# Sums of activations for w_down's Strassen parts, made in gate and up and kept in DRAM

## The chip, the cores and the metric

The kernel runs on one core of one Trainium2 chip. The metric is device time in microseconds of that core, from start to end of one execution; several executions are timed and their median is given. The engines of the core run side by side, each with its own instruction stream: PE (TensorE, the matrix products), DVE (VectorE), ACT (ScalarE), POOL (GpSimd) and SP (SyncE, which here only issues transfers). ACT and POOL issue transfers as well.

## The reference

One decoder layer on 512 tokens of width 2048, in float32: a mixer (attention and gated DeltaNet, gated and merged), then the channel mixer, then a last norm. The change concerns the channel mixer:

```python
D_MODEL = 2048; SEQ = 512
D_FF = ((8 * D_MODEL // 3 + 255) // 256) * 256      # 5632
...
        h = _rmsnorm(x, norm_ffn[l]) * (1.0 + sc_f) + sh_f
        gate, up = jnp.split(h @ w_gate_up[l], 2, axis=-1)
        x = x + gt_f * ((jax.nn.silu(gate) * up) @ w_down[l])
    return _rmsnorm(x, final_norm)
```

## The kernel before

**Products.** Every float32 operand is split into a rounded high part and a remainder (`hilo` for activations, the loops over `his` and `los` for weights): ACT casts to the high part (L242, L1718), DVE subtracts it (L243, L1721), and a product takes three matmuls: high by high, high by low, low by high. In what follows "xh" and "xl" are the two parts of an activation operand, "hi" and "lo" those of a weight.

**Order of the work.** The program is a list of units. A unit has loads (`load`, on SP), a split (the casts and subtractions of its weights), matmuls, and small calls ahead and behind (`pre`, `post`). `Driver.run` takes them in turn. Beside them run chains: Python generators that are advanced one step per 12 matmuls (`GROUP = 12`, `Driver.pump`), or until a condition holds when a unit's `pre` needs their result (`ready`, `Driver.step`). PE, SP and POOL keep the order in which the program is written; ACT and DVE are put in order by the scheduler, other than those instructions that are wrapped in `behind`, which keep the written order. `load` issues on SP, `side` on POOL. All activation tiles of 128x512 come from one pool of 68 slots, "raws" (weights as loaded, and their sums) from a pool of 5, `his` and `los` from 4 each, PSUM has 8 banks.

**Gate and up.** Hidden columns come in sets. Sets 0 and 1 are plain (`gu0`, `gu_both`); sets 1 to 10 of `big` are Strassen products (`strassen`), 16 units each. In the first half (units 0 to 7) a unit has 24 matmuls, of the products m1, m6, m7 and m5; in the second half (units 8 to 15) 18, of m2, m4 and m3 (four of these units also have four transposes). A first-half unit loads three weight tiles, DVE makes three sums (`sums`, L1698), ACT casts and DVE subtracts; one of the loaded tiles is kept in `s_dram` for the second half by a transfer that ACT issues (L1720). The sums of the next unit are made in the same step and overwrite the tile that this transfer reads. The activation operands x5, x6, x7 and x3 of gate and up are sums that the chain `combine` makes during `gu_both`. The outcome, silu(gate)·up transposed, goes to `f_dram` (`turned_a`, by POOL) for 32 of the 44 blocks of 128 hidden columns, in tiles of 128x512 that hold two blocks of one half of the tokens; blocks 36 to 39 stay in slots and 32 to 35 and 40 to 43 go to `a_dram` in two parts. The chain `gated_weights` makes the gated weights of w_down for blocks 32 to 35 during the first sets: POOL loads a tile `wg`, DVE multiplies it with a row (L1897), it is split and stored in `l_dram`.

**Down.** Then w_down, in this order: `dn(36, n)` for n = 0 to 3 (plain, 192 matmuls in all), part 0 (`strassen_down(0, n)`, n = 0, 1, blocks 0 to 15), `dn(40, n)`, part 1 (`strassen_down(1, 0)` and `last_down`, which is `strassen_down(1, 1)` with 64 transposes of x2 in it), and last blocks 32 to 35 with the gated weights ("dnt": `last_set`, `token_unit`), the sum of squares and the norm. `dn_done` evicts the banks of a `dn` set with ACT ("y", L2066).

A part's seven activation operands per q (q = 0 to 3, two units of a half use one q) come from the chain `sums_down`: four tiles a11, a21, a22, a12 are loaded from `f_dram` on SP, four sums are made on DVE (L1983) and seven operands split. m1, m6, m7 and m5 are used in the first half, m2, m4 and m3 in the second. The chain is started at unit 10 of `big(10)` for part 0, and at unit 10 of `strassen_down(0, 1)` for part 1; `free(q)` lets it take the slots of q only when older operands are gone:

```python
        def free(q):
            return q < 4 and gone[ks] >= min(q + 2, 4) and (q < 3 or plain_sets[0] > 4 * ks + 3)
```

`reload_a(40..43)` brings blocks 40 to 43 back for `dn(40, n)`, eight POOL loads, at unit 10 of `strassen_down(0, 1)`. `last_weights(n)` loads eight "wl" tiles of the gated weights on SP; `last_rows` issues four POOL transfers that add z and four SP loads of the norm's rows.

Of the kernel before, what the change touches and what calls it, by code (L numbers as in the profile page):

```python
# [15 lines left out]
P = 128  # L16
# [155 lines left out]
def block_kernel(ctx: ExitStack, tc: tile.TileContext, a: dict, out):  # L172
# [65 lines left out]
    def hilo(src, name, scale=None):  # L238
        hi, lo = S(name + "h", F32R), S(name + "l", F32R)
        n = src.shape[1]  # L240
        if scale is None:
            nc.scalar.copy(hi[:, 0:n], src)  # L242
            nc.vector.tensor_tensor(lo[:, 0:n], src, hi[:, 0:n].bitcast(F32), ALU.subtract)  # L243
# [1043 lines left out]
    z_dram = dram.tile([NT, P, D], F32, name="z_dram")  # L1287
    l_dram = dram.tile([4, 4, 2, P, 512], F32, name="l_dram")
# [358 lines left out]
    def combine():  # L1647

        for q in range(4):
# [23 lines left out]
    def strassen(w, g, u, par, operand, ready, second_read, finish, freed, extra=None):  # L1673
# [53 lines left out]
        def pre(i):  # L1727
            ready(i % 8 // 2)
# [55 lines left out]
    def big(s):  # L1784
# [8 lines left out]
        def ready(q):  # L1793
# [37 lines left out]
    def strassen_down(ks, n, extra=None):  # L1831
# [3 lines left out]
        def ready(q):  # L1835
            while made[ks] <= q:
# [68 lines left out]
    turning = []  # L1905

    def turned_a(b):
# [3 lines left out]
        def one(n):  # L1911
# [11 lines left out]
            if n == 3:  # L1923
                if s < 8:
                    f_ = S("f")
                    nc.scalar.copy(f_[:], box["ps"][:])
                    side(f_dram[2 * s + b // 2, h], f_[:])
                else:
# [14 lines left out]
    down, made, maker = [[None] * 4, [None] * 4], [0, 0], [None, None]  # L1943
# [7 lines left out]

    def sums_down(ks):

        ahead = []

        def free(q):
            return q < 4 and gone[ks] >= min(q + 2, 4) and (q < 3 or plain_sets[0] > 4 * ks + 3)

        def fetch_a(q):
            v = {}  # L1960
            for name, i, h in (("a11", 8 * ks + q, 0), ("a21", 8 * ks + q, 1), ("a22", 8 * ks + 4 + q, 1), ("a12", 8 * ks + 4 + q, 0)):
                v[name] = S(name)
                load(v[name][:], f_dram[i, h])
                yield 2
            ahead.append(v)

        for q in range(4):
            if not ahead:
                yield from until(lambda: free(q))
                yield from fetch_a(q)  # L1970
                yield 5
            v = ahead.pop(0)
            more = free(q + 1)
            if more:
                fetching = fetch_a(q + 1)
            v["x7"] = S("x7")
            d = {}
            for c, dst, x, y, op in (("m7", "x7", "a11", "a21", ALU.subtract), ("m1", "a11", None, None, None),
                                     ("m5", "a21", "a22", "a21", ALU.subtract), ("m4", "a22", None, None, None),
                                     ("m6", "a11", "a11", "a21", ALU.add), ("m2", "a12", None, None, None),  # L1980
                                     ("m3", "a12", "a11", "a12", ALU.subtract)):
                if op is not None:
                    behind(nc.vector.tensor_tensor(v[dst][:], v[x][:], v[y][:], op))  # L1983
                d[c] = hilo(v[dst][:], "x")
                if op is None:
                    if more and next(fetching, None) is None:
                        more = False
                    yield
            v = None
            if more:  # L1990
                yield from fetching
            down[ks][q] = d
            made[ks] = q + 1
            yield
# [5 lines left out]
    def gu_done(s, ps):  # L2000
# [3 lines left out]
        def done(j, h):  # L2004
            if h == 0:
                return
            for h in range(2):
# [7 lines left out]
                if j == 3:  # L2015
                    side(f_dram[s, h], f[h][:])
        return done
# [59 lines left out]
    def ffn():  # L2077
# [77 lines left out]
        def last_down():  # L2155
            for i, u in enumerate(strassen_down(1, 1, turned_x2)):
# [173 lines left out]
```

## Time and profile before

| | us |
|---|---|
| median of 3 runs (2823.3 to 2823.59) | 2823.41 |
| the profiled execution | 2822.31 |
| its span, first to last instruction | 2820.5 |
| PE busy | 2737.4 (97%) |
| DVE busy | 2012.8 (71%) |
| ACT busy | 1136.7 (40%) |
| POOL busy | 245.8 (9%) |

The profiled execution has 1.8 us outside its span and lies 1.1 us under the median. PE's busy share is high throughout; the time between matmuls that waits for other engines is small beside it, and must be read stage by stage. The granted clock of PE is 1.00 in a full-speed stretch and 0.50 in a stretch at half speed.

### The profile page before, as it was taken

The numbers are of one execution on the slowest core, as the hardware profiler recorded it, in microseconds if no ns is written. First come the engines' busy times: TensorE is split into PE (matmuls) and PEld (weight loads), VectorE is DVE, ScalarE is ACT, GpSimd is POOL, SyncE is SP. The second block draws the span as 40 slices with busy tenths as digits, with TensorE's granted clock in tenths as the row PEclk, the third lists the DMA queues.
The fourth block names the chain that finished last, engine by engine and source line by source line (L and its number), as shares of the span: only waits on it lengthen the run. The fifth ranks groups of instructions, "written<-read, shape, count | busy, mean of one in ns | idle before, by whom it ended". The sixth has DMA issues, their size and how long they took to land. (4 is left out here: it accounts for less than half of the span.)

```text
span 2820.5 us, 37178 instructions
## 1 busy us (share of the span) xinstructions
PE 2737.4 (97%) x13478; PEld 2282.4 (81%) x13478; DVE 2012.8 (71%) x3114; ACT 1136.7 (40%) x1593; POOL 245.8 (9%) x324
## 2 busy tenths in 40 slices
PE   9999999999999999999999999999999997997987
PEld 7888788888888888888997888888888885785775
DVE  8784657676867456883678888777778858767754
ACT  3443333443344332232554444444444444344332
POOL 0000011002100000000001011000000020111033
PEclk9999999999999999999999999999999998998998
DMA  9896556546755468894656667656666686687697
GB/s 353 297 353 203 157 168 185 180 146 184 210 148 179 145 213 277 283 310 138 188 168 211 233 226 239 213 202 199 206 209 214 212 216 187 225 258 182 164 300 214
DMA packets 319969, 606.00 MB, mean 215 GB/s; under 512 B 42948, under 2 KB 79972, under 8 KB 319656
## 3 DMA queue, kind: packets, MB, share of 16 engines
q1 hardware_dynamic: 255544, 482.06, 52.9%
q0 software_dynamic: 27744, 63.23, 8.5%
q10 hardware_dynamic: 36496, 58.34, 5.7%
q8 instruction: 105, 1.72, 0.2%
q14 instruction: 80, 0.66, 0.1%
HBM read 505.97 MB, written 97.53 MB: 214 GB/s over the span
## 5 line engine op out<-in xcount | busy, mean ns | idle before, releaser
L267 DVE TENSOR_TENSOR lo<-raw,hi 128x1024 fp32r<-128x1024 f32 (+1 forms) x274 | 336.8, 1230 | 314.7 <-ACT hi L266 301.0
L266 ACT CAST hi<-raw 128x1024 fp32r<-128x1024 f32 (+1 forms) x274 | 285.1, 1042 | 676.4 <-DMA raw<-in_w_in_dram 133.8
L1718 ACT CAST hi<-raws 128x1024 fp32r<-128x1024 f32 (+1 forms) x336 | 302.1, 908 | 553.7 <-DVE raws L1698 268.0
L1721 DVE TENSOR_TENSOR lo<-raws,hi 128x1024 fp32r<-128x1024 f32 (+1 forms) x336 | 350.4, 1043 | 194.5 <-ACT hi L1718 192.9
L438 DVE CUSTOM_DVE_ANT_0 rawm<-rawm,cbc 128x1024 f32<-128x1024 f32 x192 | 233.8, 1236 | 10.8 <-DMA rawm<-in_w_mod_dram 10.6
L155 PE MATMUL m<-hi,xh 128*128 128x512 f32 x448 | 183.6, 410 | 29.6 <-ACT xh L242 26.8
L155 PE MATMUL m<-lo,xh 128*128 128x512 f32 x448 | 182.2, 407 | 10.1 <-DVE lo L1721 9.9
L155 PE MATMUL m<-hi,h2h 128*128 128x512 f32 x480 | 190.5, 397 | 0.0
L155 PE MATMUL m<-lo,h2h 128*128 128x512 f32 x480 | 187.4, 390 | 1.7 <-DVE lo L1721 1.6
L155 PE MATMUL m<-hi,xl 128*128 128x512 f32 x448 | 182.4, 407 | 5.4 <-DVE xl L243 5.3
L155 PE MATMUL m<-hi,h2l 128*128 128x512 f32 x480 | 187.2, 390 | 0.0
L1698 DVE TENSOR_TENSOR sums<-raws,raws 128x1024 f32<-128x1024 f32 x112 | 136.3, 1218 | 30.2 <-DMA raws<-in_w_down_dram 17.6
L1721 DVE TENSOR_TENSOR lo<-sums,hi 128x1024 fp32r<-128x1024 f32 x112 | 136.3, 1217 | 22.0 <-ACT hi L1718 21.9
L1718 ACT CAST hi<-sums 128x1024 fp32r<-128x1024 f32 x112 | 117.4, 1048 | 51.5 <-PE m L155 51.4
L155 PEld LDWEIGHTS m<-hi,xh 128*128 128x128 f32 x448 | 88.7, 198 | 51.4 <-ACT xh L242 30.2
L155 PEld LDWEIGHTS m<-lo,xh 128*128 128x128 f32 x448 | 88.9, 198 | 32.5 <-DVE lo L1721 13.9
L155 PE MATMUL wo<-mh,hi 128*128 128x512 f32 (+1 forms) x320 | 111.2, 347 | 0.0
L155 PE MATMUL wo<-mh,lo 128*128 128x512 f32 (+1 forms) x320 | 111.0, 347 | 0.0
L155 PE MATMUL wo<-ml,hi 128*128 128x512 f32 (+1 forms) x320 | 110.9, 347 | 0.0
L155 PEld LDWEIGHTS m<-hi,xl 128*128 128x128 f32 x448 | 88.0, 197 | 27.6 <-DVE xl L243 9.6
L155 PEld LDWEIGHTS m<-lo,h2h 128*128 128x128 f32 x480 | 90.3, 188 | 21.2 <-DVE lo L1721 3.6
L155 PEld LDWEIGHTS m<-hi,h2l 128*128 128x128 f32 x480 | 90.1, 188 | 19.2
(521 smaller groups left out, 6896.2 us busy)
## 6 DMA issues: line engine op xcount, KB each, us to landing
raws<-in_w_gate_up_dram SPq DMA_DIRECT2D x400, 256.0 KB, 3.6
rawm<-in_w_mod_dram SPq DMA_DIRECT2D x192, 512.0 KB, 5.5
raw<-in_w_in_dram SPq DMA_DIRECT2D x144, 512.0 KB, 4.6
raws<-in_w_down_dram SPq DMA_DIRECT2D x160, 256.0 KB, 5.1
s_dram<-raws ACTq DMA_DIRECT2D x112, 256.0 KB, 2.2
raws<-s_dram SPq DMA_DIRECT2D x112, 256.0 KB, 3.7
raw<-in_w_o_dram SPq DMA_DIRECT2D x40, 512.0 KB, 4.3
rawa<-in_w_in_dram SPq DMA_DIRECT2D x32, 512.0 KB, 4.1
```

The costliest lines, as they stand in the source:

```text
L155: return self.tc.keep_in_program_order(f(*args, **kwargs))
L266: nc.scalar.copy(hi[:], raw[:])
L267: (lo_eng or nc.vector).tensor_tensor(lo[:], raw[:], hi[:].bitcast(F32), ALU.subtract)
L438: r = nc.vector.tensor_tensor_reduce(raw, raw, c, 1.0, 0.0, ALU.mult, ALU.add, parts[:, k, half:half + 1])
L1698: add = lambda o, x, y: behind(nc.vector.tensor_tensor(o, x, y, ALU.add))
L1718: nc.scalar.copy(hi[:], src)
L1721: nc.vector.tensor_tensor(lo[:], src, hi[:].bitcast(F32), ALU.subtract)
```

## The change

The four sums of each q are made ahead, in a new chain `sums_ahead` that starts at unit 0 of `big(5)`: POOL loads a11, a21, a22, a12 from `f_dram` into slots as soon as they have been stored there, DVE makes the sum in the written order (`behind`), POOL stores it in a new DRAM tensor `c_sums`. Over both parts that is 32 POOL loads, 32 DVE sums and 32 POOL stores. The sums inside `sums_down` go; it now loads seven finished tiles per q on SP (56 loads instead of 32), splits them with the cast pinned to the written order (`late=True`), and does so in two groups: group 0 (m1, m6, m7, m5 of all q) and then group 1 (m2, m4, m3 of all q). A first-half unit waits for group 0 of its q, a second-half unit for group 1. The chain starts at unit 8 instead of 10, in both places.

Beside this, `reload_a(40..43)` moves from unit 10 of `strassen_down(0, 1)` to unit 13; `gated_weights` starts at unit 0 of `big(2)` instead of ahead of `big(1)`; `combine`'s casts are pinned and its step after each operand gives way once instead of twice; `last_weights(0..2)` come at units 10, 12, 14 instead of 11, 13, 15, and `last_weights(3)` is issued ahead of `last_rows` in the first "dnt" set instead of in the second. PE has 12576 rows in both kernels, ACT 1709, DVE 3004 and now 3005, SP 1360 and now 1384, POOL 307 and now 371.

```diff
-    def hilo(src, name, scale=None):
+    def hilo(src, name, scale=None, late=False):
...
-            nc.scalar.copy(hi[:, 0:n], src)
+            cast = nc.scalar.copy(hi[:, 0:n], src)
+            if late:
+                behind(cast)
...
             for name in ("x3", "x6", "x7", "x5"):
-                comb[q][name] = hilo(res.pop(name)[:], name)
-                yield 2
+                comb[q][name] = hilo(res.pop(name)[:], name, late=True)
+                yield
...
-        def ready(q):
-            while made[ks] <= q:
+        def ready(q, second):
+            while made[ks][second] <= q:
                 drv.step(maker[ks])
...
+    def sums_ahead():
+
+        for ks in range(2):
+            for q in range(4):
+                def get(i, h):
+                    assert (8 * ks + i, h) in stored
+                    v = S("a")
+                    side(v[:], f_dram[8 * ks + i, h])
+                    return v
+
+                def put(i, o, x, y, op):
+                    behind(nc.vector.tensor_tensor(o[:], x[:], y[:], op))
+                    side(c_sums[ks, q, i], o[:])
+
+                yield from until(lambda: all((8 * ks + i, h) in stored for i in (q, 4 + q) for h in range(2)))
+                a11, a21 = get(q, 0), get(q, 1)
+                yield 3
+                x7 = S("x7")
+                put(2, x7, a11, a21, ALU.subtract)
+                x7 = None
+                a22 = get(4 + q, 1)
+                yield 3
+                put(0, a21, a22, a21, ALU.subtract)
+                put(1, a11, a11, a21, ALU.add)
+                a22 = a21 = None
+                a12 = get(4 + q, 0)
+                yield 3
+                put(3, a12, a11, a12, ALU.subtract)
+                a11 = a12 = None
+                summed_ahead.add((ks, q))
+                yield 2
...
     def sums_down(ks):
...
+        def source(c, q):
+            if c in ("m1", "m2", "m4"):
+                return f_dram[8 * ks + (q if c == "m1" else 4 + q), int(c == "m4")]
+            return c_sums[ks, q, ("m5", "m6", "m7", "m3").index(c)]
+
+        queue = []
+
+        def make():
+            g, q, c, v = queue.pop(0)
+            down[ks][q][c] = hilo(v[:], "x", late=True)
+            if c in ("m5", "m3"):
+                made[ks][g] = q + 1
+
+        for g, cs in enumerate((("m1", "m6", "m7", "m5"), ("m2", "m4", "m3"))):
+            for q in range(4):
+                yield from until(lambda: gone[ks] >= (q if g == 0 else 4) and (g == 0 or q < 2 or plain_sets[0] > 4 * ks + 3))
+                for c in cs:
+                    assert (ks, q) in summed_ahead
+                    v = S("a")
+                    load(v[:], source(c, q))
+                    queue.append((g, q, c, v))
+                    v = None
                     yield
-            v = None
-            if more:
-                yield from fetching
-            down[ks][q] = d
-            made[ks] = q + 1
-            yield
+                    if len(queue) > 2:
+                        make()
+            while queue:
+                yield
+                make()
...
-                if i in (11, 13, 15):
-                    with_pre([u], lambda i=i: last_weights((i - 11) // 2))
+                if i in (10, 12, 14):
+                    with_pre([u], lambda i=i: last_weights((i - 10) // 2))
...
                 if n == 0:
-                    with_pre(us, last_rows)
-                else:
-                    with_pre(us, lambda: last_weights(3))
+                    with_pre(us, lambda: (last_weights(3), last_rows()))
...
-        drv.add(gated_weights())
         for s in range(1, 11):
             for i, u in enumerate(big(s)):
-                if (s, i) == (10, 10):
+                if s in (2, 5) and i == 0:
+                    with_pre([u], lambda s=s: drv.add(gated_weights() if s == 2 else sums_ahead()))
+                if (s, i) == (10, 8):
                     with_pre([u], lambda: maker.__setitem__(0, drv.add(sums_down(0))))
...
-                if (n, i) == (1, 10):
+                if (n, i) == (1, 13):
+                    with_pre([u], lambda: [reload_a(k) for k in range(40, 44)])
+                if (n, i) == (1, 8):
                     def start():
-                        for k in range(40, 44):
-                            reload_a(k)
                         maker[1] = drv.add(sums_down(1))
```

How the scheduler and the pools lay this out is seen in the instruction streams. In the rows a line number stands first, then the operation, the tile written, the tiles read and the size; "y" is the eviction of a `dn` set's bank, "xh" the high part of a part's operand, "hi" that of a weight.

ACT before, from the last work of `dn(36, 3)` into the first units of part 0:

```order
L242 CAST ah_20010<-aT_20005 128x512
L1718 CAST hi_20026<-raws_19865 128x1024
L1720 DMA s_dram<-raws_19865 128x512
L1718 CAST hi_20031<-sums_20020 128x1024
L242 CAST xh_20082<-x_3545_20080 128x512
L1718 CAST hi_20115<-raws_19917 128x1024
L242 CAST xh_20086<-a_3499_19892 128x512
L1720 DMA s_dram<-raws_19917 128x512
L2066 ACTIVATE y_20100<-dn_3_3533_20016,gt_ffn 128x512
L2066 ACTIVATE y_20103<-dn_3_3534_20017,gt_ffn 128x512
L2066 ACTIVATE y_20106<-dn_3_3535_20018,gt_ffn 128x512
L2066 ACTIVATE y_20109<-dn_3_3536_20019,gt_ffn 128x512
```

ACT now, the same place (the row "xh" is an operand of group 1; all sixteen casts of group 0 and three more of group 1 stand further ahead):

```order
L242 CAST ah_20218<-aT_20213 128x512
L1721 CAST hi_20234<-raws_20094 128x1024
L1723 DMA s_dram<-raws_20094 128x512
L1721 CAST hi_20239<-sums_20228 128x1024
L242 CAST xh_20264<-a_20129 128x512
L2093 ACTIVATE y_20300<-dn_3_3610_20224,gt_ffn 128x512
L2093 ACTIVATE y_20303<-dn_3_3611_20225,gt_ffn 128x512
L2093 ACTIVATE y_20306<-dn_3_3612_20226,gt_ffn 128x512
L2093 ACTIVATE y_20309<-dn_3_3613_20227,gt_ffn 128x512
L1721 CAST hi_20315<-raws_20131 128x1024
L1723 DMA s_dram<-raws_20131 128x512
L1721 CAST hi_20320<-sums_20231 128x1024
```

The four evictions of the last `dn` set stood behind two operand casts of part 0's second q; now no cast of a first-half operand stands near them.

ACT before, at the step from `gu_both` into `big(1)` ("sl" evicts the banks of `gu_both`, "wgh" is a split of `gated_weights`, x3h, x6h, x7h, x5h are `combine`'s last operands):

```order
L1720 DMA s_dram<-raws_12740 128x512
L242 CAST x3h_13009<-x_2163_13007 128x512
L1718 CAST hi_13119<-raws_12740 128x1024
L242 CAST x6h_13037<-x_2161_13003 128x512
L242 CAST wgh_13054<-wg_12987 128x512
L242 CAST x7h_13072<-x_2162_13005 128x512
L2012 ACTIVATE sl_13082<-gu_2082_12519 128x256
L2012 ACTIVATE sl_13084<-gu_2082_12519 128x256
L2012 ACTIVATE sl_13082<-gu_2083_12520 128x256
L2012 ACTIVATE sl_13084<-gu_2083_12520 128x256
L242 CAST x5h_13112<-x_2160_13001 128x512
```

ACT now, at the same place:

```order
L1723 DMA s_dram<-raws_12684 128x512
L1721 CAST hi_12971<-sums_12960 128x1024
L1723 DMA s_dram<-raws_12765 128x512
L1721 CAST hi_13091<-raws_12765 128x1024
L2038 ACTIVATE sl_13058<-gu_2082_12520 128x256
L2038 ACTIVATE sl_13060<-gu_2082_12520 128x256
L2038 ACTIVATE sl_13058<-gu_2083_12521 128x256
L2038 ACTIVATE sl_13060<-gu_2083_12521 128x256
L1721 CAST hi_13096<-sums_12963 128x1024
```

The evictions "sl" stood behind five casts, of three operands, a weight and a gated weight; now they stand behind one weight cast, and the operands' casts have moved ahead of it.

POOL before, between two stores of z, in the second half of `strassen_down(0, 1)`:

```order
L155 DMA z_dram<-y_20809 128x512
L155 DMA z_dram<-euvw 128x512 x4
L155 DMA ah_21249<-a_dram 128x512
L155 DMA al_21250<-a_dram 128x512
L155 DMA ah_21253<-a_dram 128x512
L155 DMA al_21254<-a_dram 128x512
L155 DMA ah_21257<-a_dram 128x512
L155 DMA al_21258<-a_dram 128x512
L155 DMA ah_21261<-a_dram 128x512
L155 DMA al_21262<-a_dram 128x512
L155 DMA row_21265<-g_dram 128x512
L155 DMA row_21267<-g_dram 128x512
```

POOL now:

```order
L155 DMA z_dram<-euvw 128x512 x4
L155 DMA row_21396<-g_dram 128x512
L155 DMA row_21398<-g_dram 128x512
L155 DMA ah_21523<-a_dram 128x512
L155 DMA al_21524<-a_dram 128x512
L155 DMA ah_21527<-a_dram 128x512
L155 DMA al_21528<-a_dram 128x512
L155 DMA ah_21531<-a_dram 128x512
L155 DMA al_21532<-a_dram 128x512
L155 DMA ah_21535<-a_dram 128x512
L155 DMA al_21536<-a_dram 128x512
L155 DMA z_dram<-y_21613 128x512
```

The eight reloads stood ahead of the two gate rows ("row", for `strassen_down`'s outcome) and now stand behind them; they were issued 126 matmuls and more ahead of `dn(40, 0)`, and now 39 to 14 matmuls ahead of it.

DVE before, in `big(5)` around the place where the first q is summed now:

```order
L1698 TENSOR_TENSOR sums_15978<-raws_15949,raws_15950 128x1024
L1721 TENSOR_TENSOR lo_15982<-raws_15904,hi_15981 128x1024
L1698 TENSOR_TENSOR raws_15949<-sums_15978,raws_15949 128x512
L1721 TENSOR_TENSOR lo_15987<-sums_15937,hi_15986 128x1024
L1721 TENSOR_TENSOR lo_16020<-raws_15949,hi_16019 128x1024
L1721 TENSOR_TENSOR lo_16025<-sums_15978,hi_16024 128x1024
L1698 TENSOR_TENSOR raws_15990<-raws_15990,raws_15991 128x512
```

DVE now, there:

```order
L1724 TENSOR_TENSOR lo_15918<-sums_15857,hi_15917 128x1024
L1970 TENSOR_TENSOR a_15791<-a_15851,a_15791 128x512
L1724 TENSOR_TENSOR lo_15960<-raws_15869,hi_15959 128x1024
L1970 TENSOR_TENSOR a_15789<-a_15789,a_15791 128x512
L1701 TENSOR_TENSOR sums_15956<-raws_15921,raws_15922 128x1024
L1724 TENSOR_TENSOR lo_15965<-sums_15909,hi_15964 128x1024
L1701 TENSOR_TENSOR raws_15921<-sums_15956,raws_15921 128x512
L1970 TENSOR_TENSOR a_15938<-a_15789,a_15938 128x512
L1724 TENSOR_TENSOR lo_16004<-raws_15921,hi_16003 128x1024
L1724 TENSOR_TENSOR lo_16009<-sums_15956,hi_16008 128x1024
```

Three operand sums (L1970) of the first q now stand between the weight sums and subtractions. The load that the third waits for, `a_15938`, is the POOL row after the second's store, 12 matmuls ahead of it in the program.

More of the change, by code (lines that the diff above doesn't have):

```diff
@@ L1287, in block_kernel @@
     z_dram = dram.tile([NT, P, D], F32, name="z_dram")
+    c_sums = dram.tile([2, 4, 4, P, 512], F32, name="c_sums")
     l_dram = dram.tile([4, 4, 2, P, 512], F32, name="l_dram")
@@ L1941, in kept_a @@
                 side(a_dram[k - 32, i], hl[i][:].bitcast(F32))
-    down, made, maker = [[None] * 4, [None] * 4], [0, 0], [None, None]
+    down, made, maker = [[{} for _ in range(4)] for _ in range(2)], [[0, 0], [0, 0]], [None, None]
     gone, plain_sets = [0, 0, 0], [0]
@@ L1950, in until @@
             yield
-    def sums_down(ks):
[L1954 to L1973, printed above, removed]
-            if more:
[L1975 to L1987, printed above, removed]
-                    yield
-            v = None
-            if more:
-                yield from fetching
-            down[ks][q] = d
-            made[ks] = q + 1
-            yield
```

9 lines of the change are left out of this document (6 added, 3 removed).

## The prediction

> **What bounds the kernel now.** I read the page first, then the waits of PE, then a table of stretches around each place that waits, and last the timeline there.
>
> ```profile
> PE 2737.4 (97%) x13478; PEld 2282.4 (81%) x13478; DVE 2012.8 (71%) x3114; ACT 1136.7 (40%) x1593; POOL 245.8 (9%) x324
> ...
> PE m L155 <- ACT xh L242: 26.8, 7, 6.6
> PE m L155 <- DVE lo L1721: 11.5, 10, 3.3
> PE dnt L155 <- DMA wl<-l_dram: 6.0, 5, 1.5
> PE m L155 <- DVE xl L243: 5.3, 6, 1.7
> PE m L155 <- ACT sl L2012: 5.2, 1, 5.2
> ...
> PE m L155 <- ACT y L2066: 2.7, 1, 2.7
> ```
>
> PE bounds the kernel; only stretches in which it waits can be won. The waits (total, times, longest) name two that the change touches at once: 26.8 + 5.3 us for operands of w_down's parts (xh, xl), and 5.2 us for the eviction "sl" at the entrance of the Strassen sets. What they cost with the clock that falls behind them is seen in the table of stretches: length, busy time of PE, PEld, DVE, ACT, POOL, granted clock, DMA share.
>
> ```profile
> 1889.03:1932.55 43.52, 43.52 (x194) 36.05 (x192) 37.36 (x43) 18.16 (x21) 0.00 (x0) 1.00 0.70 231
> 1490.11:1541.40 51.29, 46.00 (x194) 37.24 (x193) 40.75 (x50) 22.11 (x30) 5.57 (x11) 0.93 0.63 205
> 2324.87:2394.37 69.50, 53.25 (x194) 40.99 (x192) 55.30 (x69) 31.85 (x44) 6.08 (x6) 0.85 0.68 194
> 2427.01:2474.69 47.68, 44.70 (x194) 35.71 (x192) 36.81 (x42) 16.13 (x18) 9.10 (x17) 1.00 0.83 277
> 2550.85:2623.04 72.19, 53.46 (x194) 40.60 (x192) 52.23 (x66) 29.25 (x41) 5.16 (x6) 0.83 0.62 176
> 2655.68:2706.81 51.13, 46.09 (x193) 36.76 (x192) 37.86 (x43) 16.22 (x18) 9.34 (x13) 0.97 0.90 239
> 2754.60:2808.49 53.89, 47.85 (x195) 37.17 (x193) 24.89 (x61) 16.42 (x40) 22.28 (x22) 0.90 0.79 206
> ```
>
> All rows have 192 matmuls. The first, in set 6, has no wait and sets the measure: 43.52 us, or 0.2267 us a matmul. Against it the others have too much: the entrance of big(1) 7.8 us, the first half of part 0 26.0, of its second n 4.2, part 1 28.7 and 7.6, dnt 10.4. In the two long ones DVE works 55.30 and 52.23 us, more than 43.52: even with no wait for loads it could not keep up there, since twelve sums and twenty-one remainders are made inside.
>
> **Part 0 and part 1.** ACT at the head of part 0, then DVE and SP:
>
> ```profile
> 2327.55 0.62 ACT L242 CAST xh<-x 128x512 fp32r<-128x512 f32 x1 [5.72 <-DVE x L1983]
> ...
> 2329.75 1.83 ACT L2066 ACTIVATE y<-dn,gt_ffn 128x512 f32<-128x512 f32 x3
> ...
> 2340.19 0.62 ACT L242 CAST xh<-a 128x512 fp32r<-128x512 f32 x1 [4.05 <-DVE a L1983]
> ...
> 2339.47 0.68 DVE L1983 TENSOR_TENSOR a<-a,a 128x512 f32<-128x512 f32 x1
> 2340.07 0.69 DVE L1698 TENSOR_TENSOR raws<-sums,raws 128x512 f32<-128x512 f32 x1
> 2340.84 0.69 DVE L243 TENSOR_TENSOR xl<-a,xh 128x512 fp32r<-128x512 f32 x1
> ...
> 2334.51 2.21 SPq L155 DMA_DIRECT2D raws<-in_w_down_dram  x3
> 2336.81 2.54 SPq L155 DMA_DIRECT2D a<-f_dram  x3
> ```
>
> The eviction of the last dn set waits in ACT's order behind a cast that itself waited 5.72 us for a sum; PE stands 2.73 us. Later the sums wait for loads that SP issues only at 2336.81, behind three weight loads, and PE stands 6.10 us. Now the sums are gone, and all sixteen casts of group 0 stand ahead of the part. Their cover is the end of big(10) and dn(36, n):
>
> ```profile
> 2279.40:2324.90 45.50, 45.50 (x210) 37.64 (x209) 24.23 (x31) 20.86 (x31) 19.26 (x20) 1.00 0.95 229
> ```
>
> DVE works 24 of 45.50 us there, and sixteen remainders are 16 × 0.69 = 11 us, which fit. If that cover were gone, each operand would cost its wait again. Inside the first half DVE keeps 55.30 − 12 × 0.69 − 21 × 0.69 + 8 × 0.69 = 38 us (0.69 is the row of xl; twelve sums and 21 remainders go, eight remainders of group 1 come), under 43.52. SP issues 28 operand loads for a part instead of 16, but 16 of them ahead of it; twelve more at 0.85 us each (2.54 for three) are 10 us of SP's time, beside weight loads of 24 × 0.74 = 18 us (2.21 for three).
>
> What is late next are the weights: units overwrite the tile that the transfer into s_dram reads, and DVE waits for it.
>
> ```profile
> DVE sums L1698 <- DMA s_dram<-raws: 3.5, 3, 2.4
> ...
> L1698 DVE TENSOR_TENSOR sums<-raws,raws 128x1024 f32<-128x1024 f32 x112 | 136.3, 1218 | 30.2 <-DMA raws<-in_w_down_dram 17.6
> L1721 DVE TENSOR_TENSOR lo<-sums,hi 128x1024 fp32r<-128x1024 f32 x112 | 136.3, 1217 | 22.0 <-ACT hi L1718 21.9
> ```
>
> That wait stays. A unit has 24 matmuls, 5.44 us, and DVE needs 1.22 + 0.69 + 2 × 1.22 = 4.35 us for its weights, so a wait of 2.4 us leaves up to 1.3 us late, at two or three units: I leave 3 us of the 26.0 in part 0, and 3.7 of the 28.7 in part 1, which has the same form. Gains 23 and 25. Bounds: −26 and −28.7 if nothing is left; if only the DVE surplus goes (55.30 − 43.52 = 12, 52.23 − 43.52 = 9) and the rest stays, −12 and −9. I take values near the first end, since all 13 stands of xh and xl in PE's list lie in these two stretches, with y's as the one beside them.
>
> The second n of both parts, 4.2 and 7.6 us, waits for lo (11.5 us in the list) under busy DMA (0.83 and 0.90). Nothing there is taken away; the chain for part 1 begins two units earlier and casts earlier. 0, bounds −4 to +4.
>
> **Entrance of big(1).**
>
> ```profile
> 1497.52 1.20 ACT L2012 ACTIVATE sl<-gu 128x256 f32<-128x256 f32 x4
> 1468.64 0.69 DVE L1897 TENSOR_TENSOR wg<-wg,row 128x512 f32<-128x512 f32 x1 [10.05 <-DMA wg<-in_w_down_dram]
> 1460.99 0.55 POOL L155 DMA_DIRECT2D row<-g_dram  x1 [12.70 <-DMA g_dram<-gt_ffn]
> ```
>
> DVE stood 10.05 us for the first gated weight, whose row POOL could only fetch after a store; combine's sums came late behind it, its casts stood ahead of "sl", and PE waited 5.2 us and ran at half clock after it. With gated_weights in big(2) and the casts of x in front, sl stands behind one weight cast: −7.5 of 7.8, bounds 0 and −7.8. The 10.05 us hold does not return in big(2), where the store is long done.
>
> **Gate and up.** Added: 32 sums of 0.69 us on DVE, 64 transfers on POOL. Over four sets DVE has room, ACT and POOL more:
>
> ```profile
> 1889.03:2201.35 312.32, 312.32 (x1410) 258.57 (x1408) 245.16 (x285) 138.18 (x169) 10.81 (x20) 1.00 0.62 206
> ...
> f_dram<-f POOLq DMA_DIRECT2D x28, 256.0 KB, 2.6
> wg<-in_w_down_dram POOLq DMA_DIRECT2D x16, 256.0 KB, 4.5
> ah<-a_dram POOLq DMA_DIRECT2D x8, 256.0 KB, 8.8
> a<-f_dram SPq DMA_DIRECT2D x32, 256.0 KB, 5.1
> ```
>
> The sums are 22 us in some 470, DVE goes from 78% to 83% there. But a sum holds DVE in order until its load has landed. The shortest distance in the program is 12 matmuls, 2.7 us, against 4.5 us for a POOL load (wg) and 8.8 in a busier stretch (ah): a hold of 2 to 6 us at some six places (those with 12 to 22 matmuls between). A unit's weights are made two ahead, so about one unit, 5.4 us, is spare: +2, bounds 0 and +8. The two extra transfers of 256 KB per sum, 16.8 MB in all, are 36 GB/s beside 206.
>
> By the Trainium skill (DMA: Bandwidth & Descriptors, Anatomy of one DMA), a transfer issued by GpSimd takes about 2.0 us plus its bytes at 436 GB/s, an estimate of 2.6 us for 256 KB; by it this term would be 0 and the sum 2 us lower. The same page (Issuing engine by pattern) gives simple loads to Sync as the faster way, which speaks against this change; the rows above say 4.5 us by POOL and 5.1 by SP, so here neither is shown.
>
> **Reload.** Eight POOL issues of about 0.55 us, the last pair 14 to 18 matmuls ahead of dn(40, 0), whose first two blocks are needed at its start: 39 matmuls are 8.8 us, a landing 8.8 (ah above) after up to 2.2 us of issues. +1, bounds 0 (all lands) and +5 (the fourth load lands at 8.8 + 2.2 and loses clock). z's stores behind them are needed by nobody near.
>
> **dnt.** wl waits are 6.0 us, and 0.90 of clock costs the rest of 10.4. The first three sets of wl now come one unit earlier, the fourth ahead of the norm's four loads. In the saturated tail
>
> ```profile
> wl<-l_dram SPq DMA_DIRECT2D x32, 256.0 KB, 15.2
> norm<-in_final_norm_dram SPq DMA_DIRECT2D x4, 256.0 KB, 15.9
> ```
>
> a load takes 15 us, mostly in the queue. wl(3), of which PE waited for at most 1.5 us at a time, now has the norm's four loads behind it instead of in front; the norm is later by eight loads, and weights of units 14 and 15 stand behind wl(0). −6 (the waits), bounds −10 and +4 (weights late, one stand with its clock).
>
> **Sum.** −23 − 25 + 0 − 7.5 + 2 + 1 − 6 = −58.5 on the profiled execution's 2822.31, which gives 2763.8; the median lies 1.1 us above that execution, so 2765.
>
> **Rivals.**
> 1. *The weight chain takes the place.* With operands ready, s_dram's transfers, SP's longer queue or ACT's order hold the weights, and half of the 48 us stays: 2789. For it: lo waits (11.5 us) already exist, and a stand of 2.73 us cost half clock afterwards, while one of 2.5 did not:
>
> ```profile
> 2331.70:2335.10 3.40, 3.40 (x9) 2.61 (x9) 3.31 (x4) 2.46 (x4) 3.40 (x4) 0.50 0.89 102
> 2463.40:2474.70 11.30, 8.77 (x38) 6.61 (x37) 8.95 (x11) 5.05 (x7) 0.00 (x0) 1.00 0.84 293
> ```
>
> So a few stands near 2.7 us cost 4.4 each (2.7 and half of 3.4). Against it: set 6 does the same weight work with no wait. By the Trainium skill (TensorE: Matmul & The Clock Gate, Why this matters for your kernels) only gaps above about 3 us drop the clock; by it each would cost 2.7. The trace shows the drop at 2.73, so 4.4 stands.
> 2. *Slower: sums hold DVE in gate and up.* The hold of 10.05 us before big(1) cost 7.8 us. There are 24 holds (three per q, eight q). If eight, one per q, were as long, that is 8 × 7.8 = 62 us, and the result 2765 − 2 + 62 = 2825; from nine on it is 2833 and slower. For it: POOL loads wait on stores and slots in one queue, together with gated_weights in big(5). Against it: that hold had a chain of store and row ahead of it, and of the 16 products of wg only this one waited for a load:
>
> ```profile
> L1897 DVE TENSOR_TENSOR wg<-wg,row x16: 678/684/693, 1468.6 to 1773.4; 128x512 f32<-128x512 f32 x16
> ...
>   DVE wg L1897: 10.1, 1
> ```
> 3. *The same at half size*: three or four such holds, 2788 to 2796, or a worse tail with it up to 2815.
> 4. *Nothing moves*: the operands were only the named releaser and the weights end at the same time. DVE's 55.30 us speak against it; 2823.
>
> **Chances.** The forecast (2752 to 2778) 0.62; rival 1 0.18; rival 3 0.10; rival 2 0.05; rival 4 0.02; below 2752, with all excess gone, 0.03. A difference of under 0.2% (5.6 us) is about what cannot be told from no change. Faster 0.93, same 0.02, slower 0.05. The range of eight in ten takes the forecast, rival 1 and little of rival 3, 2751 to 2798.
>
> **What would show it.** Right: no xh wait at the head of both parts and first halves near 46 us; no sl wait, big(1) 43.5 us; waits of sums L1970 for POOL loads with PE at 1.00 beside them; wl waits gone. Wrong: lo or sums waits in the parts' first halves, half clock in sets 5 to 10, x2T or norm ending the tail, dn40 beginning late.

## The result

The changed kernel takes 2788.29 us (median of 4 runs, 2781.78 to 2789.09), the kernel before 2823.36 in the same comparison: ratio of the means 0.9871, 95% interval 0.9854 to 0.9888. A second comparison on another chip gave 0.986 (0.9844 to 0.9877). The forecast was 2765 with a range of 2751 to 2798: the direction is right, the time lies inside the range, and the gain is 35 us where 58 were forecast. It lies outside the 2752 to 2778 that had most of the chance; the rivals that were let into the range hold it.

One profile is one execution, and the executions of one changed version differ by 4 to 13 us; a difference of 2 or 3 us between stretches of two runs is not secure by itself.

The page after, and PE's waits:

```profile
span 2786.4 us, 37417 instructions
PE 2719.2 (98%) x13478; PEld 2270.6 (81%) x13478; DVE 2011.2 (72%) x3114; ACT 1132.1 (41%) x1593; POOL 281.1 (10%) x388
...
PE m L155 <- DVE lo L1724: 10.3, 16, 2.1
PE m L155 <- DVE g L1806: 7.5, 4, 4.9
PE x2T L155 <- DMA x<-x_dram: 6.3, 4, 3.6
PE m L155 <- DVE euvw L1740: 3.4, 5, 2.2
```

The waits for xh, xl, sl and y are gone from the list. New are waits for g (L1806) and euvw (L1740), two evictions by DVE at the end of a Strassen set or half, and the wait for x in the second n of part 1 grew from 2.2 to 6.3 us. The stretches that answer to those of the prediction, in their order: the entrance, the first half of part 0, of its second n, of part 1, of its second n, dnt; then what follows the last matmul, and sets 5 to 10 whole.

```profile
1490.90:1534.45 43.55, 43.55 (x195) 36.06 (x194) 32.85 (x37) 16.84 (x18) 1.08 (x2) 1.00 0.62 206
2341.35:2390.45 49.10, 45.60 (x193) 37.06 (x192) 37.31 (x43) 22.30 (x29) 5.27 (x6) 0.97 0.83 247
2423.09:2468.64 45.55, 44.26 (x194) 35.83 (x192) 36.71 (x42) 16.13 (x18) 9.08 (x17) 1.00 0.84 255
2544.84:2589.91 45.07, 44.11 (x193) 35.91 (x192) 36.66 (x43) 22.24 (x30) 6.02 (x6) 1.00 0.92 262
2622.56:2671.04 48.48, 44.74 (x194) 35.75 (x192) 36.82 (x42) 16.22 (x18) 9.34 (x13) 1.00 0.89 242
2721.04:2766.02 44.98, 44.13 (x195) 35.89 (x193) 17.10 (x33) 10.74 (x29) 23.25 (x22) 1.00 0.79 187
2766.02:2786.40 20.38, 0.00 (x0) 0.00 (x0) 11.54 (x47) 10.17 (x20) 0.00 (x0) 0.63 0.52 196
1803.29:2295.68 492.39, 476.28 (x2112) 387.28 (x2111) 398.60 (x478) 214.88 (x270) 55.53 (x103) 0.99 0.73 243
```

The same sets 5 to 10, and the stretch behind the last matmul, before:

```profile
1810.95:2279.43 468.48, 468.48 (x2114) 387.86 (x2112) 367.47 (x428) 208.60 (x255) 12.97 (x24) 1.00 0.62 206
2808.49:2820.50 12.01, 0.00 (x0) 0.00 (x0) 4.76 (x19) 4.50 (x8) 0.00 (x0) 0.69 0.48 181
```

From these rows and the start times of the other stretches the account of the two profiled spans (2820.5 and 2786.4, −34.1) is:

| stretch | change, us |
|---|---|
| up to big(1) | +0.8 |
| set 1 (entrance) | −7.7 |
| sets 2 to 4 | −0.7 |
| sets 5 to 10 | +24 |
| part 0, first n / second n | −20.4 / −2.1 |
| dn(36, n) / dn(40, n) | +0.2 / 0 |
| part 1, first n / second n | −27.1 / −0.4 |
| dnt / behind the last matmul | −8.9 / +8.4 |

The parts and the entrance gave what was forecast. Two terms went wrong: gate and up took 24 us, and dnt's gain was handed back within the same 65 us. In sets 5 to 10 DVE stood for the loads of the new sums, nine times, up to 4.5 us. PE waits there mostly for evictions (g, euvw) and less for weights (lo), and the longest of these waits is at the edge of set 6:

```profile
DVE a L1970 <- DMA a<-f_dram: 14.6, 9, 4.5
...
1842.09 0.69 DVE L1970 TENSOR_TENSOR a<-a,a 128x512 f32<-128x512 f32 x1 [4.49 <-DMA a<-f_dram]
...
PE m L155 <- DVE g L1806: 7.1, 3, 4.9
PE m L155 <- DVE lo L1724: 3.6, 8, 1.2
...
1892.98 0.69 DVE L1970 TENSOR_TENSOR a<-a,a 128x512 f32<-128x512 f32 x1
1894.72 0.69 DVE L1970 TENSOR_TENSOR a<-a,a 128x512 f32<-128x512 f32 x1
...
1897.26 0.80 PE L155 MATMUL m<-hi,x5h 128*128 128x512 f32 x1 [4.92 <-DVE g L1806]
```

PE stands 16.0 us in all there, and its busy time grows by 7.8 (468.48 to 476.28); behind the stand of 4.92 us the granted clock is 0.51 from 1897 to 1901. At that edge DVE itself does not stand: it works without a pause from 1885.43, and between the set's evictions lie two of the new sums and a product and a remainder of the gated weights.

Three theories stood against each other: A, the stands of DVE for loads that are not there yet; B, the sums as extra work of DVE at the sets' edges, whatever the loads; C, the 64 added transfers.

### The profile page after: what moved, and what is told of

The parts are those of the page before. It is cut to its first block, busy times and chain, and to the rows that moved or that the text cites. A ratio compares the mean times of both kernels' runs of the same rounds, so it can differ in the third digit from the quotient of the medians.

```text
span 2786.4 us, 37417 instructions
## 1 busy us (share of the span) xinstructions
PE 2719.2 (98%) x13478; PEld 2270.6 (81%) x13478; DVE 2011.2 (72%) x3114; ACT 1132.1 (41%) x1593; POOL 281.1 (10%) x388
## 4 chain that ended last, share of the span: by engine, by line
PE 75%; DVE 11%; DMA 8%; issue 3%; ACT 2%; SPq 0%; ACTq 0%; POOL 0%; DVEq 0%; POOLq 0%
PE m L155 26%; PE wo L155 6%; PE gb L155 6%; PE v L155 4%; PE gu L155 3%; PE k L155 3%; PE s L155 3%; PE q L155 3%; PE yb L155 3%; PE z L155 3%; PE dn L155 3%; DMA raws<-in_w_down_dram 2%; DVE lo L1724 2%; PE ga L155 2%; DMA wl<-l_dram 2%
## 5 line engine op out<-in xcount | busy, mean ns | idle before, releaser
L155 PE MATMUL m<-hi,xh 128*128 128x512 f32 x448 | 176.1, 393 | 2.7 <-ACT hi L1721 2.7
L155 PE MATMUL m<-hi,xl 128*128 128x512 f32 x448 | 175.4, 392 | 0.0
L1724 DVE TENSOR_TENSOR lo<-sums,hi 128x1024 fp32r<-128x1024 f32 x112 | 136.9, 1222 | 10.5 <-ACT hi L1721 10.3
L155 PEld LDWEIGHTS m<-hi,h2h 128*128 128x128 f32 x480 | 90.4, 188 | 23.8 <-DVE euvw L1740 5.6
L155 PE MATMUL gb<-hh,hi 128*128 128x512 f32 x256 | 102.1, 399 | 0.5 <-ACT sg L1221 0.5
```

What stands on the lines that cost most here:

```text
L155: return self.tc.keep_in_program_order(f(*args, **kwargs))
L1724: nc.vector.tensor_tensor(lo[:], src, hi[:].bitcast(F32), ALU.subtract)
```

## Experiments

All ratios are against runs of the kernel before on the same chip, three rounds. "Loss" is the length of sets 5 to 10 less the 468.48 us of before.

**More steps between load and sum.** In `sums_ahead`, three places:

```diff
-                yield 3
+                yield 6
```

> The changed kernel with 6 pump steps instead of 3 between a load of sums_ahead and the sum that needs it (and after each sum), so that at least 24 more matmuls lie between them. The changed kernel lost 24 us in sets 5 to 10, against before. Theory A (DVE is held in order by sums whose POOL load has not landed, 14.6 us in nine stands): these stands go, sets 5 to 10 lose under 6 us, about 2768 us. Theory B (the sums are extra work for DVE at the edges of sets, where PE waits for a bank that DVE frees; the waits for loads do not matter): the loss stays within 8 us of 24, about 2788 or moved by a few us either way. Theory C (the 64 added transfers slow the weights' loads): the same traffic, spread out over twice the time, 2780 to 2788.

Measured: 2768.84 us, ratio 0.9816 (0.9801 to 0.9831). DVE's waits and the sets:

```profile
DVE a L1970 <- DMA a<-f_dram: 1.0, 1, 1.0
...
1798.84:2274.99 476.15, 471.55 (x2112) 386.77 (x2111) 397.40 (x478) 215.35 (x270) 55.55 (x103) 1.00 0.75 251
```

The same sums and transfers, and DVE's busy time is unchanged (397.40 against 398.60), but its stands fell from 14.6 to 1.0 us and the loss from 23.9 to 7.7. That is theory A, with 2 us more left over than it said. B and C fall as the main cause, since the work and the transfers stayed. This version is faster than the kernel before, and than the changed kernel as well, since its interval lies below both of that kernel's.

**One step more of room, and the changed kernel once more.** `yield 4` instead of 3; and the changed kernel on the same chip.

> The changed kernel with 4 pump steps instead of 3 between load and sum: at least 12 matmuls, 2.7 us, more. With 3 steps DVE stood 14.6 us for these loads and sets 5 to 10 lost 24 us, with 6 steps 1.0 us and 7.9 us. The loads land in a median of 5.5 us. Theory A (the distance decides): stands of 2 to 6 us, sets 5 to 10 lose 10 to 15 us, ratio 0.983 to 0.985. Theory B (place of the sums at the edges of sets, not the wait): stands fall as well, but the loss follows where the sums fall and may be 24 us still, ratio 0.987.

> The changed kernel as it is, once more, beside the run with 4 pump steps. Its ratio was 0.987 on another chip; every theory says 0.987 again, and stands of DVE for f_dram loads of about 15 us in sets 5 to 10.

Measured: control 0.986 (0.9844 to 0.9877), with 4 steps 0.9832 (0.9817 to 0.9846). The stands, then sets 5 to 10, of the control:

```profile
DVE a L1970 <- DMA a<-f_dram: 15.1, 8, 4.7
...
1797.57:2290.15 492.58, 475.80 (x2112) 387.20 (x2111) 398.32 (x478) 214.89 (x270) 55.51 (x103) 0.99 0.72 243
```

and with 4 steps:

```profile
DVE a L1970 <- DMA a<-f_dram: 6.1, 4, 4.2
...
1799.23:2282.94 483.71, 474.24 (x2112) 387.41 (x2111) 397.27 (x478) 214.94 (x270) 55.40 (x103) 1.00 0.73 247
```

With 3, 4 and 6 steps DVE stands 15.1, 6.1 and 1.0 us, and the loss is 24.1, 15.2 and 7.7: 9.0 us less stand are worth 8.9 us, the next 5.1 are worth 7.5. In sum a stand costs about its own length, although a unit's weights are made ahead; the table behind the next run shows that this holds in sets 7 to 10 and not in sets 5 and 6. The loss is a little above the forecast of 10 to 15 for this run.

**Without the sums.** The stored tile is one of the loaded ones; the four DVE sums of each q are left out:

```diff
-                    behind(nc.vector.tensor_tensor(o[:], x[:], y[:], op))
-                    side(c_sums[ks, q, i], o[:])
+                    side(c_sums[ks, q, i], y[:])
```

> The changed kernel without the 32 sums on DVE in sums_ahead: loads, slots and stores stay, but what is stored is one of the loaded tiles, so the operands of w_down's parts are not the sums. Theory A and B (DVE's sums cost the time, by waiting or by work): the loss of 24 us in sets 5 to 10 goes, 2764 to 2770 us. Theory C (traffic): the loss stays, 2783 to 2790.

Measured: 2768.62 us, ratio 0.9817 (0.9795 to 0.9839).

```profile
1800.82:2277.52 476.70, 471.51 (x2112) 388.32 (x2111) 378.80 (x446) 215.63 (x270) 55.26 (x103) 1.00 0.75 251
```

The loss is 8.2 us: no better than sums with room (7.7). But the two losses do not lie in the same place. Here are the losses by place, to the nearest us, with DVE's stands for the new loads; `gated_weights` still runs in sets 5 and 6 and is through in sets 7 to 10. The control repeats the first row to within 0.5 us. The last two rows are of runs further below.

| run | stands in 5, 6 | loss in 5, 6 | stands in 7 to 10 | loss in 7 to 10 |
|---|---|---|---|---|
| changed kernel | 8.9 | 17 | 5.7 | 7 |
| 4 steps | 5.5 | 13 | 0.6 | 2 |
| 6 steps | 1.0 | 5 | 0 | 2 |
| no sums | – | 8 | – | 0 |
| entrance alone | – | 3 | – | 0 |
| room and later start | 0 | 3 | 0 | 2 |

In sets 7 to 10 the account is clean: 5 us of the 7 go with the stands, one for one, 2 stay with the work of the sums, and the transfers alone cost nothing. In sets 5 and 6 it is not: 8 us are lost there without any sum, much of them at the edge of set 6, where PE stands for the same eviction with the gated weights' work, and no new sum, in front of it:

```profile
1889.59 0.50 PE L155 MATMUL m<-hi,x5h 128*128 128x512 f32 x1 [3.37 <-DVE g L1806]
```

With 6 steps that stand is 0.84 us. So part of what more room won is that the work at this edge came to lie elsewhere, and how much of the 17 us is due to stands there is not shown. B is out as the main cause, not as a small one: two sums lie in front of the 4.92 us stand, which is 1.5 us longer than without them.

**The entrance alone, in the kernel before.** `combine`'s casts pinned and one step instead of two, `gated_weights` started at big(2).

> The kernel before with one part of the change: combine's casts pinned, one step instead of two after each operand, and gated_weights started at big(2). Nothing else. Expected from the profile after: set 1 of big 76.2 us instead of 83.9 (-7.7), sets 2 and 4 -2.3 and sets 3, 5, 6 up to +5 since the gated weights now lie there; ratio 0.9975 to 0.9985. If the entrance's gain came from other parts of the change: ratio 1.000.

Measured: ratio 0.9983 (0.9974 to 0.9993). The first half of set 1, then sets 5 to 10:

```profile
1487.55:1531.10 43.55, 43.55 (x195) 36.05 (x194) 32.80 (x37) 16.85 (x18) 1.08 (x2) 1.00 0.61 206
1799.87:2271.51 471.64, 469.44 (x2112) 387.26 (x2111) 374.77 (x440) 212.57 (x263) 21.07 (x39) 1.00 0.65 213
```

The entrance is worth its 7.7 us (51.29 to 43.55 in the first half), and with no sums ahead sets 5 and 6 lose 3.2 us, because the last gated weights now lie there. So 3.2 of the 8 us were never the sums'.

**Room, and a later start.** As with 6 steps, `sums_ahead` started at unit 8 of big(6), when `gated_weights` is through:

```diff
-                if s in (2, 5) and i == 0:
+                if (s, i) in ((2, 0), (6, 8)):
```

> The changed kernel with 6 pump steps between load and sum (as in the run with more room, ratio 0.9816) and sums_ahead started at unit 8 of big(6), when gated_weights has ended, instead of unit 0 of big(5). With room, sets 5 to 10 were still 7.9 us over their 468.2. If the overlap of the two chains in sets 5 and 6 costs 4 to 5 of these (traffic of both on POOL's queue): sets 5 and 6 fall to 79.8 as in the kernel without sums ahead, ratio 0.980. If the loss goes with the sums wherever they are: it moves to sets 7 to 10, ratio 0.9815.

Measured: ratio 0.9823 (0.9805 to 0.9841), sets 5 to 10:

```profile
1800.13:2273.59 473.46, 470.33 (x2113) 387.06 (x2112) 392.32 (x470) 213.99 (x269) 49.10 (x91) 1.00 0.74 245
```

Sets 5 and 6 fell to 79.71 and 79.84 us, as in the run of the entrance alone, and the loss to 5.0; but the second half of the first n of part 0, where the last sum now lies, grew from 32.64 to 35.46:

```profile
2369.60:2405.06 35.46, 33.28 (x146) 26.80 (x144) 28.05 (x37) 13.85 (x16) 2.15 (x4) 1.00 0.63 207
...
2370.55 0.69 DVE L1970 TENSOR_TENSOR a<-a,a 128x512 f32<-128x512 f32 x1 [3.03 <-DMA a<-f_dram]
```

The whole is not faster: the first expectation came for sets 5 and 6 (79.8) and not for the ratio (0.980). The 2.8 us in part 0 are a stand of the old kind, in a new place: DVE waits 3.03 us for the last sum's load, and PE 2.0 us for an eviction behind it. The 2.7 us won in sets 5 to 10 fit an overlap of the two chains, but are too few to be secure from one profile each.

**Sums on POOL.**

```diff
-                    behind(nc.vector.tensor_tensor(o[:], x[:], y[:], op))
+                    nc.gpsimd.tensor_tensor(o[:], x[:], y[:], op)
```

> The changed kernel with the 32 sums of sums_ahead on POOL instead of DVE (the same loads, stores and slots). POOL's own products of this size took 1.3 to 1.6 us in the tail, 32 of them are 45 us beside its 281. Theory A and B: DVE is free of the sums and PE's waits in sets 5 to 10 go, 2764 to 2772 us; if POOL work slows DVE beside it, up to 2778. Theory C: 2783 to 2790.

Measured: 2778.95 us, ratio 0.9847 (0.9828 to 0.9867): between what A and B allow and what C does. Sets 5 to 10, then groups of DVE in them (busy, mean ns), here and in the run without sums:

```profile
1801.34:2289.94 488.60, 476.85 (x2112) 390.45 (x2111) 399.21 (x446) 215.65 (x270) 143.33 (x135) 0.99 0.72 245
...
L1701 DVE TENSOR_TENSOR sums<-raws,raws 128x1024 f32<-128x1024 f32 x46 | 60.6, 1317 | 2.2 <-DMA raws<-in_w_gate_up_dram 1.8
L1701 DVE TENSOR_TENSOR raws<-raws,raws 128x512 f32<-128x512 f32 x48 | 38.6, 805 | 0.0
```

```profile
L1701 DVE TENSOR_TENSOR sums<-raws,raws 128x1024 f32<-128x1024 f32 x47 | 57.3, 1218 | 4.9 <-DMA raws<-in_w_gate_up_dram 4.9
L1701 DVE TENSOR_TENSOR raws<-raws,raws 128x512 f32<-128x512 f32 x48 | 32.8, 684 | 4.2 <-DMA raws<-in_w_gate_up_dram 4.2
```

DVE has no sum of its own here, the same 446 instructions as in the run without sums, and yet works 399.21 us instead of 378.80: two-input products take 1317 ns instead of 1218 and 805 instead of 684. The 22 us that were taken off DVE came back as 20. Some POOL sums, and the DVE instructions beside the ends of two of them:

```profile
1828.91 7.18 POOL L155 TENSOR_TENSOR a<-a,a 128x512 f32<-128x512 f32 x1
...
1844.23 1.29 POOL L155 TENSOR_TENSOR a<-a,a 128x512 f32<-128x512 f32 x1 [3.46 <-DMA a<-f_dram]
...
2062.77 18.28 POOL L155 TENSOR_TENSOR x<-a,a 128x512 f32<-128x512 f32 x1 [4.54 <-DMA a<-f_dram]
...
2141.69 19.12 POOL L155 TENSOR_TENSOR x<-a,a 128x512 f32<-128x512 f32 x1 [3.79 <-DVE lo L1724]
```

```profile
1833.73 1.21 DVE L1724 TENSOR_TENSOR lo<-sums,hi 128x1024 fp32r<-128x1024 f32 x1
1835.37 1.81 DVE L1724 TENSOR_TENSOR lo<-raws,hi 128x1024 fp32r<-128x1024 f32 x1 [0.43 <-ACT hi L1721]
1837.26 2.14 DVE L1724 TENSOR_TENSOR lo<-sums,hi 128x1024 fp32r<-128x1024 f32 x1
...
2080.02 2.12 DVE L1701 TENSOR_TENSOR sums<-raws,raws 128x1024 f32<-128x1024 f32 x1
```

A POOL sum takes 1.29 us where DVE pauses, but 7.18, 18.28 and 19.12 us where DVE works back to back; the one of 18.28 us ends beside the first DVE instruction in that row that is longer than the others of its kind (2.12 us instead of 1.21). DVE's subtraction goes from 1.21 to 1.81 and 2.14 us where DVE had paused for 0.43 us and POOL was adding. The Trainium skill (SBUF — State Buffer, SBUF: two separate sides) says that DVE with two SBUF inputs and GpSimd contend for one port pair, which either holds for a whole instruction while the other blocks; these rows agree (18.28 and 2.12 us above). The expectation allowed 6 us for such a slowing. DVE's longer instructions are not the whole of this run's loss of 20.1 us, though: with 6 steps DVE was as busy (397.40 us) and the loss was 7.7. PE waits here at the edges of two halves (3.8 us for euvw, 3.7 for g) and 4.2 us for remainders; what makes each late is not taken apart.

**Grouping without sums ahead.** No `sums_ahead`; the four sums of each q are made on DVE in `sums_down` ahead of the part, group 0 first; only x3 goes through `c_sums`. Core of the edit:

```diff
+            a11, a21, a22, a12 = ahead.pop()
+            x7 = S("x7")
+            total(x7, a11, a21, ALU.subtract)
+            split(q, "m1", a11)
...
+            total(a12, a11, a12, ALU.subtract)
+            split(q, "m6", a11)
+            side(c_sums[ks, q, 3], a12[:])
```

> Nothing in gate and up: no sums_ahead. sums_down makes group 0 (m1, m6, m7, m5) of all q in front of the part from four tiles of f_dram per q, with the sums on DVE there, makes x3 as well and keeps only that in c_sums; group 1 within the part as in the changed kernel. Both groups stay in front of and within the part, so this tells whether the gain at the parts comes from the grouping or from sums made early. If from the grouping: sets 5 to 10 return to 78.08 us each (-24), part 0 and part 1 keep first halves of 45 to 50 us, 2764 to 2770. If DVE has no room in the stretch ahead of a part (71 of about 80 us by count): first halves 55 to 65 us and 2780 to 2800.

Measured: 2794.1 us, ratio 0.9908 (0.9892 to 0.9924). First halves of part 0 and part 1:

```profile
2318.62:2372.39 53.77, 47.15 (x194) 37.49 (x192) 43.04 (x53) 24.97 (x33) 7.14 (x8) 0.94 0.85 256
2535.07:2588.43 53.36, 47.45 (x194) 37.49 (x192) 39.83 (x48) 22.23 (x29) 6.78 (x8) 0.90 0.85 252
```

Sets 7 to 10 are back at 78.08 and 77.85 us, as expected; the halves are a little under the 55 to 65 expected for the second case, and waits for xh (1.9 us) and xl (2.4) are back in part 0. The two parts take 362.3 us, before 385.0, in the changed kernel 334.9. So this saves 24 in gate and up less the gated weights' 3, and gives 27 back at the parts: grouping, with the earlier start and the pinned casts, is worth 23 of the 50 us without early sums.

**Sums ahead without grouping.** All seven operands of a q before the next q, with before's condition:

```diff
-        for g, cs in enumerate((("m1", "m6", "m7", "m5"), ("m2", "m4", "m3"))):
...
+        for q in range(4):
+            yield from until(lambda: gone[ks] >= min(q + 2, 4) and (q < 3 or plain_sets[0] > 4 * ks + 3))
+            for c in ("m1", "m6", "m7", "m5", "m2", "m4", "m3"):
```

> The changed kernel (sums made ahead in gate and up) without the two groups: sums_down takes all seven finished operands of a q before the next q, with the condition that before had (only q 0 and 1 in front of the part, and only as slots come free). If early sums alone make the gain of the parts (DVE's work inside is down by 8 us, and no sum waits for a load): first halves about 47 to 52 us, ratio about 0.987 as in the changed kernel. If the grouping is needed (operands still arrive behind weight loads within the first half): first halves 55 to 65 us, some 10 to 25 us longer in both parts together, ratio 0.991 to 0.996.

Measured: 2791.7 us, ratio 0.9896 (0.9881 to 0.9912).

```profile
2338.22:2388.29 50.07, 46.02 (x194) 37.02 (x193) 41.03 (x49) 26.41 (x36) 6.12 (x6) 0.97 0.84 244
2545.53:2591.68 46.15, 44.29 (x193) 35.81 (x192) 37.08 (x44) 24.71 (x35) 6.02 (x6) 1.00 0.92 259
```

First halves of 50.07 and 46.15 us, near the 49.10 and 45.07 of the changed kernel; the parts together take 339.8 us against 334.9. So early sums, with the earlier start and the pinned casts, give 45 of the 50 us, grouping on top of them 5. The ratios agree that something is left: 0.9896 against 0.986 (0.9844 to 0.9877) of the changed kernel on the same chip. The expectation of "about 0.987" was too good by those 5.

**The norm's loads first.** `last_rows` ahead of `last_weights(3)`:

```diff
-                    with_pre(us, lambda: (last_weights(3), last_rows()))
+                    with_pre(us, lambda: (last_rows(), last_weights(3)))
```

> The changed kernel with the norm's loads (and z's transfers) ahead of the last eight wl loads, in the same call, as the order was before; nothing else. The changed kernel's dnt takes 45.0 us and then 20.4 us pass to the end, before it was 53.9 and 12.0. Theory D (the end is set by the chain of token rows, which begins when the norm lands): the norm lands some 13 us earlier, the end comes 5 to 8 us earlier, ratio 0.984 to 0.985. Theory E (one full queue: what one load gains another loses): dnt waits for wl again, about 6 us more there, 6 us less after it, ratio 0.987 within 0.001.

Measured: ratio 0.987 (0.9854 to 0.9887). dnt and what follows it:

```profile
2723.82:2779.01 55.19, 49.03 (x195) 37.89 (x193) 25.30 (x61) 16.42 (x40) 22.26 (x22) 0.91 0.78 201
2779.01:2790.60 11.59, 0.00 (x1) 0.00 (x0) 4.74 (x19) 4.50 (x8) 0.00 (x0) 0.63 0.50 186
...
PE dnt L155 <- DMA wl<-l_dram: 6.1, 5, 1.5
```

66.8 us in all, 65.4 in the changed kernel (45.0 + 20.4), 65.9 before (53.9 + 12.0). With the norm first PE waits 6.1 us for wl; with wl first DVE waits for the norm and the rows of the last tokens come late:

```profile
DVE x2t L2243 <- DMA norm<-in_final_norm_dram: 8.5, 1, 8.5
```

This is theory E: the transfers are dense from 2690 to 2750 (DMA share 1.08 in the changed kernel), and an order among them only says who is late.

## Why the prediction was right, and where it was wrong

- **Entrance**, forecast −7.5, measured −7.7, alone as well (0.9983, less the 3 us of the gated weights).
- **Part 0 and part 1**, −23 and −25; measured −20.4 and −27.1 in the profile, and −2.1 and −0.4 in the second n, forecast 0. That DVE's work in the half goes from 55 to 38 us was right (37.31). What is late next are the weights, as said: PE waits 2.7 us for a hi cast in part 0, and DVE's sums wait 2.3 to 2.5 us for s_dram ahead of it.

```profile
PE m L155 <- ACT hi L1721: 2.7, 1, 2.7
...
2347.90 1.23 DVE L1701 TENSOR_TENSOR sums<-raws,raws 128x1024 f32<-128x1024 f32 x1 [2.33 <-DMA s_dram<-raws]
```

- **Reload**, +1; measured 0, dn(40, n) is 43.68 us in both.
- **Gate and up**, +2 with bounds 0 and +8: the failed term. Measured +24. Some 16 of them go with more room between load and sum, and as many without the sums; 3.2 come from the gated weights' later start, which the prediction put at nothing; of the last 4 or 5, 2 stay with the sums' work in sets 7 to 10, and the rest is open. The holds of DVE were seen, with 12 matmuls as the shortest distance, and their size too: 2 to 6 us at six places were forecast, 14.6 us in nine came. The step that failed is the price, "about one unit, 5.4 us, is spare". That reserve is one of weights, and of the 16.0 us that PE stands only 3.9 are for weights (lo, hi). The other 12.1 are for evictions at the ends of sets and halves (g, euvw), which that reserve does not cover; 10.5 of them are DVE's, which is busy 81% of the time there. In sets 7 to 10 a stand of DVE then costs its full length. The third rival (half the size of the slower one, 2788 to 2796, chance 0.10) is what came, though through many stands of 0.3 to 4.5 us and not three or four of ten. The time alone would fit the first rival (2789) as well; only the stretches tell them apart.
- The POOL load's time: the row for `a<-f_dram` now gives the median directly:

```profile
a<-f_dram POOLq DMA_DIRECT2D x32, 256.0 KB, 5.5
```

It is 5.5 us, between the rows used (4.5 and 8.8), and twice the 2.6 us that an estimate by the Trainium skill's formula gave (DMA: Bandwidth & Descriptors, Anatomy of one DMA). Had loads landed in 2.6 us, a distance of 12 matmuls (2.7 us) would have left hardly a stand. The prediction saw no difference between loads by POOL and by SP in its rows (4.5 and 5.1 us), which came from different stretches. In sets 5 to 10 of the changed kernel, side by side, loads of 256 KB by SP landed in a median of 4.0 us (weights) and 4.9 (six from `f_dram`), those by POOL in 5.5; no run issues the new loads on SP.
- **dnt**, −6: it gained 8.9, and 8.4 of it were lost behind the last matmul. The prediction noted that the norm comes later by eight loads, and gave it no price of its own: that is the step left out.
- **Rival 1** (the weights keep half of the 48 us) did not come; rivals 2 and 4 neither.
- **Luck**: the range holds the time because it reached up to 2798 for the first rival, which did not come. Of the signs of being wrong, half clock in set 6 (0.96 on the mean of the set) and a late norm did come.

## What to carry to other kernels

A sum that was moved out of a critical stretch into one with spare engine time is nearly free only if its operands are there when its turn comes: in an order that is kept, the distance from load to use, set against the landing time that the trace shows, is most of the price, and the work the smaller part (5 and 2 us in sets 7 to 10). What such a stand delays is to be asked of everything behind it in that order, evictions too, and not only of the products with a reserve. In a stretch where the transfer queue is full, moving one load ahead must be priced with the load that it overtakes. Work given to POOL is not off DVE's account while both read two operands: here 20 of 22 us came back.

## What the runs showed of the hardware

That POOL and DVE get in each other's way was expected, its size was not. Over sets 5 to 10 two groups of DVE's instructions with two inputs became 8% (1218 to 1317 ns) and 18% (684 to 805 ns) longer on the mean, and DVE's busy time rose by 20 us in all, nearly the whole relief. A POOL sum took 1.3 us alone and up to 19.1 us beside DVE's unbroken work, so POOL was the one that waited longer.
